# Lower priority for the broadcast of the norms' reciprocal roots

## The chip, the cores and the metric

The kernel runs on one core of a Trainium2 chip. The metric is the device time of one execution in microseconds. Five engines work side by side, each through its own list of instructions: TensorE (PE), VectorE (DVE), ScalarE (ACT), GpSimd (POOL), and SyncE (SP), which here only issues DMAs. An engine takes its instructions strictly in the order of its list; an instruction that waits for a semaphore holds everything behind it on that engine.

## The reference

One decoder layer in float32 over 2048 prompt positions and 8 sample positions (2056 columns), width 1024:

```
h = rmsnorm(x, g_mix);  u, v = split(h @ w_in)                # 1024 -> 512 + 512
y_s5   = glu(gelu(scan_of_complex_state(u)))                  # S5 head group
y_pool = (trailing means of v, windows 2/4/8/16, minus v) @ pool_w * pool_scale
x = x + concat(y_s5, y_pool) @ w_out
h = rmsnorm(x, g_ffn);  x = x + (gelu(gate) * val) @ w_down   # gate, val: causal conv of h @ w_up
y = rmsnorm(x, g_final)
rmsnorm(x, g) = x * rsqrt(mean(x*x, axis=-1) + 1e-6) * g
```

Outputs are y and the new states, in float32.

## The kernel before

The columns of x (positions) lie along the free dimension, the features along the 128 partitions. So a norm needs for each column one number, the reciprocal root of the mean square, in all 128 partitions. `rstd_bcast` (L104 to L123) makes it for a stretch of n columns from the sums of squares, which lie as a 128 x nb tile (position in the partition, block of 128 positions in the column; nb is 2 to 4). VectorE, and ScalarE for the root, work out `rs_r` = the reciprocal root with one Newton step (L110 to L116). Then for each block b VectorE multiplies the identity by the column b of `rs_r`, which gives a diagonal tile `rs_d` (L121, two buffers), and TensorE multiplies a tile of ones by it (L122), which puts the block's numbers as a row into every partition of the PSUM tile `ps_rb`. At last ScalarE copies the n columns of `ps_rb` to SBUF (L123, `rstd`, `rs` or `rs_last`).

This happens 21 times: 5 times in the preparation of x for the input projection (`prep_x`, L253 and L255: stretches of 512, 512, 512, 264 and 256 columns, called SUB 0 to SUB 4 below), 8 times after the out-projection (`norm_out` L946, and L938 for the last stretch), 8 times in the final norm (`final` L1332).

Each fp32 matmul of a projection is done as three matmuls of high and low halves: `mm3` (L87 to L89: high x high, low of the activations x high weights, high x low). The halves are split by ScalarE (a cast, `xh` L79, `wh` L75) and by VectorE or GpSimd (the difference, `xl` L80, `wl` L76). `prep_x` loads `xraw` (three buffers from SUB 2 on), splits it with the gain multiplied in, and gathers the sums of squares.

The stages follow each other: the input projection with the pooling heads and the start of the S5 scan (0 to about 300 us), gates and out-projection with the second half of the scan (to about 600 us), the up-projection of the FFN (to about 1505 us), the down-projection with the final norms (to the end).

The order in which each engine's list is written comes from a scheduler that takes, among the instructions whose inputs would be ready, the one with the lowest priority number. The number (`tc.cur_priority`) counts up by one with every instruction the program emits. Background work, the S5 scan that runs beside the projections, is emitted with BGO = 50 added (`back` L765 to L770 and `s5_ahead` L772 to L777), so that it falls behind foreground work emitted up to 50 instructions later.

Of the kernel before, what the change touches and what calls it, by code (L numbers as in the profile page):

```python
# [40 lines left out]
BGO = 50  # L41
# [3 lines left out]
def build(tc, a):  # L45
# [3 lines left out]
    with es:  # L49
# [54 lines left out]
        def rstd_bcast(ssum, out, n):  # L104
            nb = (n + 127) // 128
            v = misc.tile([128, 8], F32, tag="rs_v", name="rs_v")
            s = misc.tile([128, 8], F32, tag="rs_s", name="rs_s")
            r = misc.tile([128, 8], F32, tag="rs_r", name="rs_r")
            v, s, r = v[:, :nb], s[:, :nb], r[:, :nb]
            V.tensor_scalar(out=v, in0=ssum, scalar1=1.0 / D, scalar2=EPS, op0=ALU.mult, op1=ALU.add)  # L110
            S.activation(out=s, in_=v, func=AF.Sqrt)
            V.reciprocal(out=r, in_=s)
            V.tensor_tensor(out=s, in0=r, in1=r, op=ALU.mult)
            V.tensor_tensor(out=s, in0=s, in1=v, op=ALU.mult)
            V.tensor_scalar(out=s, in0=s, scalar1=-0.5, scalar2=1.5, op0=ALU.mult, op1=ALU.add)
            V.tensor_tensor(out=r, in0=r, in1=s, op=ALU.mult)  # L116
            ps = psm[0].tile([128, 512], F32, tag="ms", name="ps_rb")
            for b in range(nb):
                w = min(128, n - b * 128)
                dg = misc.tile([128, 128], F32, tag="rs_d", name="rs_d")  # L120
                V.tensor_scalar(out=dg[:, :w], in0=ident[:, :w], scalar1=r[:, b:b + 1], scalar2=None, op0=ALU.mult)  # L121
                T.matmul(ps[:, b * 128:b * 128 + w], lhsT=ones, rhs=dg[:, :w], start=True, stop=True)  # L122
            S.copy(out=out, in_=ps[:, :n])  # L123

        def rstd_from(accs, out, n):
            nb = (n + 127) // 128
            ps = psm[0].tile([128, 512], F32, tag="ms", name="ps_st")
            if n % 128:
                V.memset(ps[:, 0:nb], 1.0)
            for b in range(nb):  # L130
                w = min(128, n - b * 128)
                for x, acc in enumerate(accs):
                    T.matmul(ps[0:w, b:b + 1], lhsT=acc[:, b * 128:b * 128 + w], rhs=ones[:, 0:1],
                             start=x == 0, stop=x == len(accs) - 1)
            rstd_bcast(ps[:, 0:nb], out, n)
# [39 lines left out]
        with ExitStack() as er_:  # L175
# [37 lines left out]
            def prep_x(i):  # L213
# [38 lines left out]
                if nat:  # L252
                    rstd_bcast(st(None), rs[:, :n], n)  # L253
                else:
                    rstd_from([acc[:, :n]], rs[:, :n], n)  # L255
# [1226 lines left out]
```

## Time and profile before

| | |
|---|---|
| three runs | 1993.02, 1995.8 (median), 1999.92 us |
| the profiled execution | 1997.34 us, its span 1995.5 us |
| mean granted TensorE clock | 0.973 |
| PE busy | 1877.3 us, 94% of the span |
| DVE, ACT, POOL busy | 1404.4, 898.1, 904.7 us |

The span is the time from the first to the last record of the trace; the 1.84 us between it and the time lie around it. The granted clock is given as a share of full speed. A timeline row gives the start, the duration, the instruction as "out<-in" by the program's names, and in brackets how long its engine was idle before it and what released it. Matmuls overlap, so their pace is read from the distance of their starts, not from their durations.

### The profile page before, as it was taken

How to read it: one execution, taken by the hardware profiler on the slowest of the kernel's cores; microseconds unless marked ns; L12 is line 12 of the kernel's file. 1: busy time of each engine (PE TensorE's matmuls, PEld its weight loads, DVE VectorE, ACT ScalarE, POOL GpSimd, SP SyncE). 2: the span in 40 equal slices, each digit the busy share in tenths (PEclk: the TensorE clock that was granted, in tenths of full speed). 3: DMA queues.
4: the chain of work that ended last, by engine and by line, in shares of the span. 5: the costliest groups of instructions: out<-in, count | busy, mean ns of one | idle time of the engine just before them, and what ended most of it. 6: DMA issues, size and time to landing. Idle time of an engine off the chain costs nothing.

```text
span 1995.5 us, 38363 instructions
## 1 busy us (share of the span) xinstructions
PE 1877.3 (94%) x14680; PEld 1815.0 (91%) x14680; DVE 1404.4 (70%) x2423; ACT 898.1 (45%) x1666; POOL 904.7 (45%) x1091
## 2 busy tenths in 40 slices
PE   6888997999998999999997999999998999999998
PEld 4667876999988999999997999999998989999997
DVE  8888576875588777787789777777775343444675
ACT  5333224544445555555565555555554332322332
POOL 4365662211156455445457555445531165134651
PEclk9989998999999999999998999999998999999999
DMA  6456666865453433233334233323317574356663
GB/s 218 159 165 176 189 179 214 224 176 154 130 178 115 132 122 117 91 112 101 96 102 142 90 114 99 100 87 117 97 60 267 173 248 147 103 189 212 227 205 120
DMA packets 214215, 296.61 MB, mean 149 GB/s; under 512 B 41216, under 2 KB 157824, under 8 KB 213776
## 3 DMA queue, kind: packets, MB, share of 16 engines
q1 hardware_dynamic: 201104, 285.76, 45.3%
q10 hardware_dynamic: 12928, 8.41, 1.5%
q8 instruction: 115, 1.88, 0.4%
q14 instruction: 68, 0.56, 0.1%
HBM read 199.60 MB, written 93.32 MB: 147 GB/s over the span
## 4 chain that ended last, share of the span: by engine, by line
PE 55%; POOL 4%; DVE 4%; DMA 3%; issue 3%; ACT 1%; DVEq 0%; POOLq 0%; ACTq 0%; SPq 0%
PE ps_X L1147 8%; PE ps_X L1146 8%; PE ps_X L1145 8%; PE ps_d L88 4%; PE ps_d L87 4%; PE ps_d L89 4%; PE ps_Z L1146 4%; PE ps_Z L1147 4%; PE ps_Z L1145 4%; PE ps_Y L1147 2%; PE ps_Y L1145 2%; PE ps_Y L1146 2%; DMA x_d<-xo 1%; DMA wr<-w_dn 1%; POOL xo L1307 1%
## 5 line engine op out<-in xcount | busy, mean ns | idle before, releaser
L87 PE MATMUL ps_d<-bh,wh 128*128 128x256 f32 (+1 forms) x1232 | 346.0, 285 | 12.5 <-ACT bh L75 12.5
L88 PE MATMUL ps_d<-bl,wh 128*128 128x256 f32 (+1 forms) x1232 | 349.3, 285 | 6.3 <-DVE bl L76 6.3
L89 PE MATMUL ps_d<-bh,wl 128*128 128x256 f32 (+1 forms) x1232 | 348.5, 284 | 0.0
L76 DVE TENSOR_TENSOR wl<-raw,wh 128x512 fp32r<-128x512 f32 x308 | 270.5, 881 | 64.0 <-ACT wh L75 61.5
L75 ACT CAST wh<-raw 128x512 fp32r<-128x512 f32 x308 | 189.7, 619 | 236.7 <-PE ps_X L1146 166.8
L1173 DVE SCALAR_TENSOR_TENSOR ps_cv<-hup,cst,ps_cv 128x512 f32<-128x512 f32 x352 | 258.1, 750 | 53.1 <-ACT ps_cv L1171 50.9
L1080 POOL TENSOR_TENSOR raw<-raw 128x512 f32<-128x512 f32 x176 | 241.4, 1372 | 83.7 <-DVE wl L76 68.3
L87 PEld LDWEIGHTS ps_d<-bh,wh 128*128 128x128 f32 x1232 | 233.1, 191 | 13.5 <-ACT bh L75 13.5
L88 PEld LDWEIGHTS ps_d<-bl,wh 128*128 128x128 f32 x1232 | 234.7, 191 | 7.4 <-DVE bl L76 7.4
L89 PEld LDWEIGHTS ps_d<-bh,wl 128*128 128x128 f32 x1232 | 235.0, 191 | 0.0
L76 DVE TENSOR_TENSOR bl<-br,bh 128x1536 fp32r<-128x1536 f32 (+3 forms) x56 | 112.4, 2008 | 101.0 <-ACT bh L75 94.0
L1171 ACT ACTIVATE ps_cv<-hup,cst 128x512 f32<-128x512 f32 x176 | 135.9, 782 | 8.3 <-DVE hup L1133 3.9
L87 PE MATMUL ps_in<-xh,wh 128*128 128x512 f32 (+2 forms) x288 | 110.0, 383 | 10.4 <-ACT xh L79 8.1
L926 POOL TENSOR_TENSOR acc<-acc,sq 128x256 f32<-128x256 f32 (+1 forms) x56 | 44.5, 794 | 150.9 <-ACT sq L925 148.6
L88 PE MATMUL ps_in<-xl,wh 128*128 128x512 f32 (+2 forms) x288 | 106.0, 368 | 6.7 <-DVE xl L80 6.7
L1100 POOL TENSOR_TENSOR tt<-cv 128x256 f32<-128x256 f32 (+1 forms) x88 | 79.8, 915 | 61.6 <-DVE cv L1180 28.0
L75 ACT CAST bh<-br 128x1536 fp32r<-128x1536 f32 (+3 forms) x56 | 76.6, 1376 | 66.5 <-PE ps_d L89 65.9
L89 PE MATMUL ps_in<-xh,wl 128*128 128x512 f32 (+2 forms) x288 | 104.3, 363 | 0.1
L1147 PE MATMUL ps_X<-b11h,wl 128*128 128x256 f32 (+1 forms) x352 | 100.0, 284 | 3.1 <-DVE wl L76 3.1
L1146 PE MATMUL ps_X<-b11l,wh 128*128 128x256 f32 (+1 forms) x352 | 99.9, 284 | 2.9 <-DVE b11l L76 2.9
L1145 PE MATMUL ps_X<-bt2h,wh 128*128 128x256 f32 (+1 forms) x352 | 99.9, 284 | 2.5 <-ACT p L1128 2.5
L1146 PE MATMUL ps_Y<-b21l,wh 128*128 128x256 f32 (+1 forms) x352 | 99.3, 282 | 2.5 <-DVE b21l L76 2.5
(436 smaller groups left out, 6476.5 us busy)
## 6 DMA issues: line engine op xcount, KB each, us to landing
raw<-w_up SPq DMA_DIRECT2D x176, 256.0 KB
wr<-w_dn SPq DMA_DIRECT2D x36, 704.0 KB
op_d<-tt SPq DMA_DIRECT2D x33, 512.0 KB
br<-op_d SPq DMA_DIRECT2D x21, 768.0 KB
br<-op_d SPq DMA_DIRECT2D x21, 640.0 KB
op_d<-cv SPq DMA_DIRECT2D x33, 256.0 KB
wr<-w_in SPq DMA_DIRECT2D x16, 512.0 KB
tab<-tab_d SPq DMA_DIRECT2D x32, 256.0 KB
```

The lines of the kernel that those rows point to most:

```text
L75: S.copy(out=hi, in_=src)
L76: (eng or V).tensor_tensor(out=lo, in0=src, in1=hi.bitcast(F32), op=ALU.subtract)
L87: T.matmul(ps, lhsT=wh, rhs=rh, start=k == 0, stop=False)
L88: T.matmul(ps, lhsT=wh, rhs=rl, start=False, stop=False)
L89: T.matmul(ps, lhsT=wl, rhs=rh, start=False, stop=k == K - 1)
L1080: P.tensor_tensor(out=r, in0=x, in1=y, op=op)
L1100: P.tensor_tensor(out=o, in0=x, in1=y, op=ALU.subtract)
L1145: T.matmul(ps, lhsT=wh[:, k], rhs=hh[:, k], start=first and k == 0, stop=False, skip_group_check=not first)
L1146: T.matmul(ps, lhsT=wh[:, k], rhs=hl[:, k], start=False, stop=False, skip_group_check=not first)
L1147: T.matmul(ps, lhsT=wl[:, k], rhs=hh[:, k], start=False, stop=k == 3, skip_group_check=not first)
L1171: S.activation(out=c, in_=h[:, o:o + 512], func=AF.Identity, scale=tap(2, jj), bias=col(C_CB, jj))
L1173: V.scalar_tensor_tensor(out=c, in0=h[:, o - 2 + k:o + 510 + k], scalar=tap(k, jj), in1=c, op0=ALU.mult, op1=ALU.add)
```

## The change

In `rstd_bcast` the PSUM tile, the diagonal tiles, the broadcast matmuls and ScalarE's copy are emitted with the background's 50 added to the priority, and then the counter is set back to where it stood before these instructions. Nothing that is computed changes, and no instruction is added or taken away.

```diff
             V.tensor_tensor(out=r, in0=r, in1=s, op=ALU.mult)
+            p_ = tc.cur_priority
+            tc.cur_priority = p_ + BGO
             ps = psm[0].tile([128, 512], F32, tag="ms", name="ps_rb")
             for b in range(nb):
                 w = min(128, n - b * 128)
...
                 V.tensor_scalar(out=dg[:, :w], in0=ident[:, :w], scalar1=r[:, b:b + 1], scalar2=None, op0=ALU.mult)
                 T.matmul(ps[:, b * 128:b * 128 + w], lhsT=ones, rhs=dg[:, :w], start=True, stop=True)
             S.copy(out=out, in_=ps[:, :n])
+            tc.cur_priority = p_
 
         def rstd_from(accs, out, n):
```

So the scheduler writes the lists in another order. TensorE's list differs in two stretches only, rows 363 to 703 (about 130 to 230 us of the trace before) and rows 1164 to 2075 (about 300 to 430 us), and by two matmuls of the down-projection that change places. The broadcasts of SUB 0 and SUB 1 stand where they stood; of the 16 later ones two change their place between the matmuls around them (the first and the second after the out-projection). Names with a line number in the changed kernel are 2 higher at L121 to L123 and 3 higher from there on.

TensorE, input projection, before: blocks 3 and 4 of SUB 2's norm (`ps_rb` from `rs_d` 1424 and 1427) stand in the middle of a unit of the projection (`ps_in` 1477).

```order
L88 MATMUL ps_in_1477<-xl_378,wh_1186 128x512
L89 MATMUL ps_in_1477<-xh_377,wl_1187 128x512
L87 MATMUL ps_in_1477<-xh_386,wh_1186 128x512
L122 MATMUL ps_rb_1417<-rs_d_1424,ones_132 128x128
L122 MATMUL ps_rb_1417<-rs_d_1427,ones_132 128x128
L88 MATMUL ps_in_1477<-xl_387,wh_1186 128x512
L89 MATMUL ps_in_1477<-xh_386,wl_1187 128x512
L87 MATMUL ps_in_1477<-xh_395,wh_1186 128x512
```
Now at this place stand blocks 1 and 2 (1418 and 1421), which before stood some 30 rows earlier:

```order
L89 MATMUL ps_in_1477<-xh_386,wl_1187 128x512
L87 MATMUL ps_in_1477<-xh_395,wh_1186 128x512
L88 MATMUL ps_in_1477<-xl_396,wh_1186 128x512
L124 MATMUL ps_rb_1417<-rs_d_1418,ones_132 128x128
L89 MATMUL ps_in_1477<-xh_395,wl_1187 128x512
L87 MATMUL ps_in_1477<-xh_404,wh_1186 128x512
L124 MATMUL ps_rb_1417<-rs_d_1421,ones_132 128x128
L88 MATMUL ps_in_1477<-xl_405,wh_1186 128x512
```
and blocks 3 and 4 stand behind the next unit's (`ps_in` 1626) fourth and fifth tile:

```order
L87 MATMUL ps_in_1626<-xh_1362,wh_1616 128x512
L88 MATMUL ps_in_1626<-xl_1363,wh_1616 128x512
L124 MATMUL ps_rb_1417<-rs_d_1424,ones_132 128x128
L89 MATMUL ps_in_1626<-xh_1362,wl_1617 128x512
L87 MATMUL ps_in_1626<-xh_1371,wh_1616 128x512
L124 MATMUL ps_rb_1417<-rs_d_1427,ones_132 128x128
L88 MATMUL ps_in_1626<-xl_1372,wh_1616 128x512
```
What moved: blocks 3 and 4 went 23 and 25 rows back, behind the rest of `ps_in` 1477, a matmul of the pooling heads (`ps_z` 1512) and eleven matmuls of the next unit. SUB 3's last block (`rs_d` 1610) goes back as well, from row 446 to row 473.

VectorE beside it, before: both diagonal tiles stand ahead of the split of SUB 2's sixth tile (`xl` 1381); `xl` of L80 are the splits, `rt` and `ra` a table for the scan, `pl`, `vt`, `csum` the pooling heads.

```order
L673 SCALAR_TENSOR_TENSOR pl_1294<-wsum_1292,vt_1286 128x512
L279 TENSOR_TENSOR ra_1305<-rt_1304,ns_680 128x4x32 x2
L280 TENSOR_TENSOR rt_1304<-rt_1304,nc_679 128x8x32
L121 TENSOR_SCALAR rs_d_1424<-ident_145,rs_r_1409 128x128
L121 TENSOR_SCALAR rs_d_1427<-ident_145,rs_r_1409 128x128
L80 SCALAR_TENSOR_TENSOR xl_1381<-xraw_1378,cst_134,xh_1380 128x512
L676 TENSOR_TENSOR pl_1294<-wsum_1292,icn_285 128x16
```
Now the split 1381 follows on `rt` at once, and seven rows on the diagonal tiles stand behind the eighth tile's split (`xl` 1399):

```order
L665 SCALAR_TENSOR_TENSOR csum_1460<-ones_132,vt_1456 128x528
L80 SCALAR_TENSOR_TENSOR xl_1390<-xraw_1387,cst_134,xh_1389 128x512
L285 TENSOR_TENSOR rt_1304<-rt_1304,ra_1305 128x4x64 x2
L80 SCALAR_TENSOR_TENSOR xl_1399<-xraw_1396,cst_134,xh_1398 128x512
L123 TENSOR_SCALAR rs_d_1424<-ident_145,rs_r_1409 128x128
L676 SCALAR_TENSOR_TENSOR pl_1464<-wsum_1462,vt_1456 128x512
L123 TENSOR_SCALAR rs_d_1427<-ident_145,rs_r_1409 128x128
```
What moved: the two diagonal tiles went behind the splits 1381, 1390 and 1399. SUB 3's last one (1610) now stands behind `xl` 1588, the last split of SUB 3; before it stood ahead of six of the eight.

ScalarE in the out-projection, before: `wo` are weights that are cast, `yg` the scan's activation, `sg` the sigmoid of the gate that frees a PSUM tile, `gh` the high halves for the out-projection.

```order
L75 CAST wo0h_3207<-wo0r_3205 128x1024
L606 COPY bus_280<-psw_3472 128x32
L639 ACTIVATE yg_3498<-psy_3499 128x544
L75 CAST wo1h_3213<-wo1r_3211 128x1024
L898 ACT_TABLE_LOAD
L898 ACTIVATE sg_3294<-ps_g_3281 128x256
L898 ACTIVATE sg_3314<-ps_g_3301 128x256
L75 CAST gh4_3259<-zr_3257 128x256
```
Now a weight's cast stands ahead of `yg`, and two casts `gh` stand ahead of the sigmoids:

```order
L75 CAST wo0h_3207<-wo0r_3205 128x1024
L609 COPY bus_280<-psw_3472 128x32
L75 CAST wo1h_3213<-wo1r_3211 128x1024
L642 ACTIVATE yg_3498<-psy_3499 128x544
L75 CAST gh4_3259<-zr_3257 128x256
L75 CAST gh5_3265<-zr_3263 128x256
L901 ACT_TABLE_LOAD
L901 ACTIVATE sg_3294<-ps_g_3281 128x256
L901 ACTIVATE sg_3314<-ps_g_3301 128x256
```
What moved: `gh4` and `gh5` went ahead of the first sigmoid. At the next stretch of columns the two casts go ahead as well, a square and a cast of another kind too, and a second pair of table load and `yg` now stands between the last sigmoid and `gh3`.

## Rows read from the trace of the kernel before

**Rows 1.** The page: span, and TensorE's busy time.
```profile
span 1995.5 us, 38363 instructions
...
PE 1877.3 (94%) x14680; PEld 1815.0 (91%) x14680; DVE 1404.4 (70%) x2423; ACT 898.1 (45%) x1666; POOL 904.7 (45%) x1091
```

**Rows 2.** Windows: length, PE, PEld, DVE, ACT, POOL busy, PEclk, DMA share, GB/s.
```profile
140.00:150.00 10.00, 7.41 (x22) 5.75 (x23) 10.00 (x20) 4.41 (x8) 7.22 (x4) 0.66 0.87 273
170.00:180.00 10.00, 8.21 (x60) 7.07 (x59) 8.55 (x19) 4.69 (x8) 1.71 (x4) 1.00 0.49 148
200.00:250.00 50.00, 50.00 (x333) 43.95 (x333) 26.91 (x46) 11.22 (x19) 31.87 (x41) 1.00 0.66 186
320.00:330.00 10.00, 6.71 (x33) 5.92 (x33) 9.39 (x19) 7.39 (x17) 2.12 (x1) 0.78 0.72 241
```

**Rows 3.** Waits of PE, 300 to 640 us: total us, times, longest.
```profile
PE ps_rb L122 <- DVE rs_d L121: 8.0, 3, 4.8
PE psy L638 <- DVE H L619: 4.0, 1, 4.0
PE ps_g L87 <- ACT sg L898: 3.1, 3, 2.1
```

**Rows 4.** Timeline of PE: start us, us, instruction, [idle before <- releaser].
```profile
138.07 0.40 PE L89 MATMUL ps_in<-xh,wl 128*128 128x512 f32 x1
138.30 0.39 PE L87 MATMUL ps_in<-xh,wh 128*128 128x512 f32 x1
142.59 1.22 PE L122 MATMUL ps_rb<-rs_d,ones 128*128 128x128 f32 x4 [3.89 <-DVE rs_d L121]
143.46 0.77 PE L88 MATMUL ps_in<-xl,wh 128*128 128x512 f32 x1
...
147.87 0.48 PE L89 MATMUL ps_in<-xh,wl 128*128 128x512 f32 x1
```

**Rows 5.** Timeline of DVE beside it (same columns).
```profile
140.18 2.55 DVE L121 TENSOR_SCALAR rs_d<-ident,rs_r 128x128 f32<-128x128 f32 x2
...
144.46 0.16 DVE L677 TENSOR_TENSOR pl<-pl,vt 128x16 f32<-128x16 f32 x1
...
148.38 1.24 DVE L114 TENSOR_TENSOR rs_s<-rs_s,rs_v 128x2 f32<-128x2 f32 x1
149.54 0.74 DVE L80 SCALAR_TENSOR_TENSOR xl<-xraw,cst,xh 128x512 fp32r<-128x512 f32 x1
150.20 0.47 DVE L121 TENSOR_SCALAR rs_d<-ident,rs_r 128x128 f32<-128x128 f32 x2
```

**Rows 6.** Timeline of POOL beside it.
```profile
138.23 4.22 POOL L76 TENSOR_TENSOR wl<-wr,wh 128x1024 fp32r<-128x1024 f32 x1 [1.33 <-ACT wh L75]
...
147.29 2.31 POOL L665 TENSOR_TENSOR wsum<-csum 128x512 f32<-128x512 f32 x1 [0.16 <-DVE csum L662]
```

**Rows 7.** All rs_d, durations ns min/median/max, first and last start.
```profile
L121 DVE TENSOR_SCALAR rs_d<-ident,rs_r x51: 231/280/2357, 35.9 to 1987.6; 128x128 f32<-128x128 f32 x48, 128x8 f32<-128x8 f32 x3
```

**Rows 8.** Last split of the preparation: DVE, PE; waits of ACT, 128 to 176.
```profile
176.03 0.49 DVE L80 SCALAR_TENSOR_TENSOR xl<-xraw,cst,xh 128x256 fp32r<-128x256 f32 x1
...
176.57 0.38 PE L88 MATMUL ps_in<-xl,wh 128*128 128x256 f32 x1 [0.21 <-DVE xl L80]
...
ACT xh L79 <- DMA xraw<-xT: 27.5, 15, 4.4
```

**Rows 9.** PE in the out-projection, at a wait for the sigmoid.
```profile
321.44 0.39 PE L87 MATMUL ps_g<-yh,wg3h 128*128 128x256 f32 x1 [2.13 <-ACT sg L898]
```

**Rows 10.** ACT in the out-projection, next stretch: table load, yg, gh.
```profile
348.57 1.28 ACT L639 ACT_TABLE_LOAD   x1
349.86 0.63 ACT L639 ACTIVATE yg<-psy 128x544 f32<-128x544 f32 x1
350.38 0.40 ACT L75 CAST gh<-zr 128x256 fp32r<-128x256 f32 x1
```

**Rows 11.** PE at a later broadcast, in the out-projection.
```profile
583.17 1.19 PE L122 MATMUL ps_rb<-rs_d,ones 128*128 128x128 f32 x4 [4.82 <-DVE rs_d L121]
```

## Prediction

> **What bounds the kernel now.** I read the head of the page first. TensorE is busy for 1877.3 us of a span of 1995.5 us [rows 1], so all that any order of work can give back is the 118 us in which it idles, and the stretches in which its clock is down. The windows show where that is. From 200 to 250 us TensorE has no idle time (50.00 of 50) at full clock; in 140 to 150 us it is busy for 7.41 of 10 us at a mean granted clock of 0.66, and in 320 to 330 us for 6.71 at 0.78 [rows 2]. Then I read the waits of TensorE, since the change touches only what TensorE waits for at `ps_rb`, and whatever moves around it. In the out-projection and at its end the broadcasts cost three waits of 8.0 us together, the longest 4.8 [rows 3]; in the input projection the timeline has one of 3.89 us [rows 4]. Of the other waits of the out-projection, 4.0 us go to the scan (`psy` on `H`) and 3.1 us to the sigmoids (`ps_g` on `sg`) [rows 3].
>
> Last I compared these places with the new lists. The wait of 3.89 us stands at blocks 3 and 4 of SUB 2's norm, which move. The one of 4.8 us [rows 11] stands at a broadcast after the out-projection that keeps its neighbours on every engine, and so do the other two of the 8.0 us. The change can therefore touch two stretches: the input projection around 130 to 230 us, by the wait itself, and the out-projection around 300 to 430 us, by the order that results there. The FFN keeps its order but for two matmuls that change places.
>
> **Input projection: what goes.** TensorE starts the last matmul before the broadcast at 138.30 and the broadcast at 142.59, after 3.89 us of idling for `rs_d` [rows 4]. VectorE has both diagonal tiles in hand from 140.18 for 2.55 us [rows 5], where the median of one is 280 ns and the longest of all 51 is 2357 ns [rows 7]: this is the one that was held up, and it ends with GpSimd's `wl`, which runs from 138.23 for 4.22 us [rows 6]. After the wait the clock is down: eleven matmuls start 0.44 us apart (from 143.46 to 147.87), where before it they start 0.23 us apart (138.07, 138.30) [rows 4]. That loses 11 x 0.21 = 2.3 us. Gross, 3.9 + 2.3 = 6.2 us are at stake here.
>
> **What comes instead.** TensorE now runs through the place of the wait. After 138.30 it does eleven more matmuls and two broadcast blocks (the old pair took 0.87 us, 142.59 to 143.46, at the low clock [rows 4], so 0.45 at the full one), and so comes to the pooling matmul `ps_z` 1512 at about 138.3 + 2.5 + 0.5 = 141.3. `ps_z` needs the last instruction on `pl` 1294 (144.46, 0.16 us [rows 5]). VectorE's list up to it is 2.55 us shorter by the two diagonal tiles [rows 5], so that `pl` is ready at 142.1 and TensorE waits 0.8 us. With `ps_z` (512 columns of the same kind as the pair's 256, so twice its 0.45) and eleven matmuls (2.5) it stands at block 3 at 145.5. The diagonal tile is ready later: it stands behind the split 1399, which was at 149.54 [rows 5]. Of what was ahead of that split the two diagonal tiles (2.55) go, and so do the small instructions of the next norm, of which the step at 148.38 took 1.24 us [rows 5]: 3.8 together. The tile ends at 149.54 - 3.8 + 0.74 + 0.28 [rows 5, 7] = 146.8, a wait of 1.3 us. The next tile stands one pooling instruction further, about a split's 0.74 us [rows 5], of which one matmul covers 0.23: another 0.5. New waits: 0.8 + 1.3 + 0.5 = 2.6 us. They come in three pieces instead of one, and I take the clock as not falling. At about 147 us TensorE would be 6.2 - 2.6 = 3.6 us ahead.
>
> **How much of it lasts.** SUB 3's last block (`rs_d` 1610) now stands behind the last split of SUB 3, `xl` 1588, so TensorE idles there for some 3 to 4 us that it did not idle before. This is not simply a cost: the matmuls behind it need the splits of SUB 3 and SUB 4 anyway. The end of the whole preparation is the split at 176.03, for which TensorE waits at 176.57, the last such wait [rows 8]; what decides is when that split comes. It hangs on ScalarE, which waits for the loads [rows 8], and a load starts when a split has freed one of three buffers. The splits move up by the 2.55 us of the two diagonal tiles [rows 5], and the loads with them. In 170 to 180 us TensorE still idles for 1.8 us [rows 2], so the lead is not capped by its own work there, and from 200 us on it is full [rows 2], so the lead stays. I take 2.5 us of gain, the shift of the splits, rather than the lead of 3.6, which the wait for the last split caps. The bounds: the whole 6.2 us are gained if the new waits fall where TensorE would wait anyway; at the other end the loads do not move up and the new wait at `rs_d` 1610 is a second one of 3.9 us with its 2.3 us of low clock: 6.2 - 2.6 - 6.2, a loss of 2.6 us.
>
> Here the Trainium skill speaks. Its page "SBUF — State Buffer", section "Who interferes with whom", has it that a `tensor_scalar` of VectorE can enter a mode in which it needs the ports that it shares with GpSimd, and that whoever began first holds them for its whole instruction. The rows agree: the 2357 ns tile ends with `wl`. By that rule the moved tile is not safe either, since it stands close behind `csum`, with which GpSimd's `wsum` begins (147.29, 2.31 us long [rows 6]); it would be held for what is left of `wsum` once the two splits between them (0.74 each [rows 5]) are done, at most 2.31 - 1.48 = 0.8 us. By the rule the gain would be 2.5 - 0.8 = 1.7 us, by the pair at 150.20, which took 0.47 us for two tiles with no GpSimd work beside it in the trace [rows 5], 2.5 us.
>
> **Out-projection.** Here no broadcast that moves has a wait of its own; the second one even moves up. What changes is ScalarE's order. Two casts `gh`, 0.40 us each [rows 10] and overlapping by 0.1, now precede the sigmoid for which TensorE waits 2.13 us at 321.44 [rows 9]: +0.7 us. At the next stretch a square and a copy also precede it, +0.4 to +1.1. Against this the scan's matmuls and VectorE's steps stand some 5 us earlier, of whose 4.0 us wait [rows 3] a part goes. I take zero, between -4.0 and +4.
>
> **The sum.** The profiled execution took 1997.34 us, 1.84 us more than its span [rows 1]. 1997.34 - 2.5 + 0 = 1994.8; the median of the runs shown lies 1.5 us below the profiled one, so a typical run is expected between 1993.3 and 1994.8. I say 1994.
>
> **Rivals.**
> (a) Faster than that. The order around the broadcast was the cause of both losses, and they go: 6.2 us in the input projection, and in the out-projection half of the 7.1 us of waits for the scan and the sigmoids [rows 3], 3.5 us. 1997.3 - 9.7 = 1987.6. For it: the clock of 0.66 [rows 2] is a loss that only the wait explains. Against it: the new place of block 3 still lies ahead of its diagonal tile.
> (b) Slower, by ScalarE in the out-projection. The sigmoid frees the PSUM tile that `ps_g` needs; the casts put ahead cost 0.7 us at the first stretch and 1.1 at the next, and there a table load and a `yg`, 1.28 + 0.63 us [rows 10], now stand ahead of `gh3`, the last input of the first `ps_o`: 1.9. Together 3.7 us; each of two such waits is followed by matmuls at the lower clock as after the wait at 142 us, 2 x 2.3 = 4.6. With no gain in the input projection: 1997.3 + 8.3 = 2005.6. It decides from the point at which the wait before `ps_g` at 321.44 grows above 3 us. For it: the mean clock there is already 0.78 [rows 2]. Against it: ScalarE idles in that stretch for a quarter of the time (7.39 of 10 busy [rows 2]).
> (c) The change hardly does what it says. 5 of 21 broadcasts move, none of them one that the 8.0 us [rows 3] are lost at, and the preparation stays bound by its loads: 1996 to 1998.
>
> **The numbers.** Forecast 0.45, (a) 0.25, (b) 0.15, (c) 0.15. About 0.3%, 6 us, is what a measurement of this kernel can tell from no change. Faster by more than that (under 1989.8): 0.22 of (a) and 0.08 of the forecast's tail, 0.30. Slower (over 2001.8): 0.13 of (b), 0.05 from the tails of the forecast and (c), 0.18. The same: 0.52. The likeliest case alone spans 1990 to 1999; the range reaches to most of (a) and of (b), 1985 to 2004.
>
> **What would show it.** Right: no wait over 3 us at `ps_rb` before 150 us, one of 1 to 2 us at 145 to 148, the clock of that stretch at about 0.9, and the split now at 176.03 at about 173.5. Wrong: a broadcast's wait of 3 us or more at a lower clock at about 160 us, that split at 176 or later, or waits of `ps_g` for `sg` that add up to more than 5 us. All of it is wrong if the FFN, whose order stands, differs by more than 2 us between the traces.

## The result and the profile after

The changed kernel takes 2007.1 us (median of 7 runs, 2002.06 to 2014.19), the kernel before 1993.28 us (7 runs, 1991.29 to 1999.92): a ratio of 1.0071, 95% interval 1.0055 to 1.0087. It is slower by about 14 us, above the range. The profiled execution took 2002.06 us, the lowest of its seven, its span 1.86 us less.

Ahead of everything else stands where on the way it falls behind. The first matmul of each stage marks it (us from the span's start; gates and out-projection begin with `ps_g`, the up-projection with `ps_X`, the down-projection with `ps_d`):

| | first `ps_g` | first `ps_X` | first `ps_d` | end |
|---|---|---|---|---|
| before | 298.4 | 598.7 | 1512.9 | 1995.5 |
| after | 300.4 | 607.8 | 1524.7 | 2000.2 |
| later by | 2.0 | 9.1 | 11.8 | 4.7 |

So between these two traces 2.0 us are lost in the input projection and 7.1 in the out-projection. The 2.0 are rather too little: in the six traces whose input projection has the order of before (before, and e8, e10, e11, e12, e14 of the experiments below) the first `ps_g` stands at 294.3 to 298.4 us, on average at 296.3; in the nine with the changed order (after, e3, e7, e9, e13, e15 to e18) at 297.8 to 301.5, on average at 299.7, which is 3.4 us later. The FFN's order is the same but for two matmuls that change places; the up-projection took 912.1 to 918.0 us over the twenty traces of this study, so its 2.7 are within what it varies by. The last stage took 482.6 us in the trace before, the longest of all; the others have 475.6 to 481.0. That stage alone brings these two spans from 11.8 us apart to 4.7; the medians lie 13.8 apart.

The page after, span and TensorE [rows 1]:

```profile
span 2000.2 us, 38361 instructions
...
PE 1873.6 (94%) x14680; PEld 1813.7 (91%) x14680; DVE 1410.1 (70%) x2423; ACT 898.8 (45%) x1666; POOL 901.9 (45%) x1091
```
TensorE works 3.7 us less than before and idles 8.4 us more. The windows after (columns as in [rows 2]), with two more stretches, 165 to 174 and 340 to 360 us:

```profile
140.00:150.00 10.00, 5.28 (x22) 3.38 (x20) 10.00 (x18) 2.04 (x4) 5.12 (x4) 1.00 0.91 272
...
165.00:174.00 9.00, 8.26 (x56) 8.26 (x57) 8.25 (x17) 3.29 (x8) 1.27 (x1) 0.81 0.34 95
...
170.00:180.00 10.00, 9.40 (x74) 8.84 (x72) 9.88 (x20) 3.70 (x8) 1.41 (x3) 0.99 0.38 110
...
320.00:330.00 10.00, 5.27 (x21) 4.55 (x21) 9.91 (x18) 8.74 (x17) 2.35 (x1) 0.66 0.87 274
...
340.00:360.00 20.00, 14.15 (x108) 13.54 (x107) 13.13 (x23) 9.86 (x17) 8.61 (x11) 0.95 0.59 176
```
and these two before:

```profile
165.00:174.00 9.00, 6.91 (x49) 5.95 (x48) 8.86 (x15) 4.15 (x10) 0.82 (x3) 1.00 0.36 105
...
340.00:360.00 20.00, 19.27 (x164) 19.05 (x162) 13.75 (x29) 12.39 (x24) 9.21 (x11) 1.00 0.71 198
```
In 140 to 150 us the clock is back at 1.00 from 0.66 (about 0.9 was forecast), and yet TensorE gets as many matmuls done as before, 22: its busy time shrank because each is shorter, and idle time took the place. But this trace is alone in that: over 140 to 152 us the other eight with the changed order have a clock of 0.72 to 0.86, and the six with the order of before 0.72 to 0.86 as well. And in 165 to 174 us the clock is down, 0.81 from 1.00; it is at 0.62 to 0.81 there in six of the nine with the changed order, and at 1.00 in five of the six with the order of before. In 340 to 360 us TensorE gets 108 matmuls done instead of 164.

**Input projection.** TensorE after (start, duration, instruction, idle time before it):

```profile
144.58 1.13 PE L700 MATMUL ps_z<-pl,pw__287 128*128 128x512 f32 x2 [2.97 <-DVE pl L680]
...
150.28 0.49 PE L124 MATMUL ps_rb<-rs_d,ones 128*128 128x128 f32 x2 [2.04 <-DVE rs_d L123]
...
165.74 0.39 PE L124 MATMUL ps_rb<-rs_d,ones 128*128 128x8 f32 x2 [2.40 <-DVE rs_d L123]
```
The wait of 3.89 us at 142.59 [rows 4] is gone; three stand for it, 7.4 us together, and the low clock of 165 to 174 us comes behind the last of them. VectorE beside it, and then GpSimd:

```profile
140.51 2.85 DVE L80 SCALAR_TENSOR_TENSOR xl<-xraw,cst,xh 128x512 fp32r<-128x512 f32 x1
...
144.37 0.16 DVE L680 TENSOR_TENSOR pl<-pl,vt 128x16 f32<-128x16 f32 x1
...
147.54 1.83 DVE L285 TENSOR_TENSOR rt<-rt,ra 128x256 f32<-128x256 f32 x2
149.29 0.74 DVE L80 SCALAR_TENSOR_TENSOR xl<-xraw,cst,xh 128x512 fp32r<-128x512 f32 x1
149.96 0.28 DVE L123 TENSOR_SCALAR rs_d<-ident,rs_r 128x128 f32<-128x128 f32 x1
```
```profile
138.52 4.29 POOL L76 TENSOR_TENSOR wl<-wr,wh 128x1024 fp32r<-128x1024 f32 x1 [1.29 <-ACT wh L75]
...
147.12 1.64 POOL L668 TENSOR_TENSOR wsum<-csum 128x512 f32<-128x512 f32 x1 [1.86 <-DVE csum L665]
```
The diagonal tiles are no longer held up: all 51 take 225 to 1318 ns, median 281, where the longest took 2357 [rows 7]. But the split that took their place in VectorE's list takes 2.85 us instead of its usual 0.74: it ends 0.55 us behind GpSimd's `wl` (142.81), as the first of the tiles ended 0.08 us behind it before (142.45) [rows 5, 6]. The same happens a second time. Before, the small `rs_s` at 148.38 took 1.24 us and ended with GpSimd's `wsum` [rows 5, 6]; now `rs_s` is gone from there, and two `rt`, which took 0.75 us before, take 1.83 while `wsum` runs. So `pl` comes at 144.37 as before (144.46), and the split that was at 149.54 at 149.29: hardly anything moved up. The end of the preparation moves back, from 176.03 [rows 8] to 178.43, with TensorE waiting for it:

```profile
178.43 0.49 DVE L80 SCALAR_TENSOR_TENSOR xl<-xraw,cst,xh 128x256 fp32r<-128x256 f32 x1
```
```profile
178.97 0.39 PE L88 MATMUL ps_in<-xl,wh 128*128 128x256 f32 x1 [0.36 <-DVE xl L80]
```
It is SUB 2's move that does this: that split stands at 177.99 in e1, where SUB 2 alone moves, and at 174.41 in e2, where SUB 3 alone does.

**Out-projection.** TensorE's waits after, 300 to 640 us (total, times, longest), against [rows 3]:

```profile
PE ps_rb L124 <- DVE rs_d L123: 11.2, 4, 4.7
PE ps_g L87 <- DVE x L923: 5.9, 3, 4.7
PE psy L640 <- ACT yg L642: 4.2, 2, 2.8
PE psy L641 <- DVE H L622: 4.0, 1, 4.0
...
PE ps_g L87 <- ACT sg L901: 1.5, 1, 1.5
```
The sigmoids cost less than before (1.5 for 3.1). Two things are new, `ps_g` on the residual add `x`, which frees its PSUM tile, and a wait at the first broadcast after the out-projection, which had none before. The longest of the one, and the other:

```profile
357.70 0.41 PE L87 MATMUL ps_g<-yh,wg2h 128*128 128x256 f32 x1 [4.75 <-DVE x L923]
...
393.68 0.68 PE L124 MATMUL ps_rb<-rs_d,ones 128*128 128x128 f32 x4 [2.51 <-DVE rs_d L123]
```
To see where the wait for `x` comes from one follows it back through the engines. SyncE (start, duration of the issue) before, and after:

```profile
334.66 0.37 SPq L866 DMA_DIRECT2D wo5r<-w_out  x1
336.63 1.26 SPq L566 DMA_DIRECT2D tab<-tab_d  x2
...
343.13 0.33 SPq L866 DMA_DIRECT2D wo7r<-w_out  x1
```
```profile
337.16 0.61 SPq L569 DMA_DIRECT2D tab<-tab_d  x1
337.87 1.45 SPq L869 DMA_DIRECT2D wo5r<-w_out  x1
...
348.52 0.33 SPq L869 DMA_DIRECT2D wo7r<-w_out  x1
```
A load of the scan's table now stands ahead of the weight `wo5r`, which is issued 3.2 us later; 2.0 of these are the later start of the stage. ScalarE after, then VectorE after and before:

```profile
344.98 1.05 ACT L75 CAST wo5h<-wo5r 128x1024 fp32r<-128x1024 f32 x1 [8.86 <-DMA wo5r<-w_out]
...
346.56 0.17 ACT L609 COPY bus<-psw 128x32 f32<-128x32 f32 x1
...
356.84 0.62 ACT L642 ACTIVATE yg<-psy 128x544 f32<-128x544 f32 x1
```
```profile
346.75 0.69 DVE L603 TENSOR_TENSOR t<-psw,tab 64x512 f32<-64x512 f32 x1 [6.64 <-ACT bus L609]
347.46 0.68 DVE L604 TENSOR_TENSOR t<-psw,tab 64x512 f32<-64x512 f32 x1
348.18 0.42 DVE L923 TENSOR_TENSOR x<-ps_o,xt 128x256 f32<-128x256 f32 x1
...
357.22 0.42 DVE L923 TENSOR_TENSOR x<-ps_o,xt 128x256 f32<-128x256 f32 x1
```
```profile
344.01 0.75 DVE L920 TENSOR_TENSOR x<-ps_o,xt 128x256 f32<-128x256 f32 x2 [4.89 <-DMA xt<-xT]
344.69 1.23 DVE L76 TENSOR_TENSOR wo6l<-wo6r,wo6h 128x1024 fp32r<-128x1024 f32 x1
347.62 0.42 DVE L920 TENSOR_TENSOR x<-ps_o,xt 128x256 f32<-128x256 f32 x1 [1.70 <-DMA xt<-xT]
348.07 0.69 DVE L600 TENSOR_TENSOR t<-psw,tab 64x512 f32<-64x512 f32 x1
```
Before, ScalarE's cast of `wo5` starts at 339.60. After, it waits 8.86 us for the load; the scan's `bus` stands behind it, the scan's steps `t` on VectorE wait for `bus`, and the residual adds stand among and behind these steps, where before they stood ahead of them. The add at 357.22 is the one for which TensorE idles 4.75 us; `yg`, at 349.86 before [rows 10], comes at 356.84. The scan's steps themselves are no later than before (346.75 against 348.07, the second pair 353.62 against 354.71): what changed for the adds is that they stand behind these steps. Some 1.8 of the 4.75 us are two small steps `gx` just ahead of the add, which take 1.46 and 0.67 us beside GpSimd's `wo7l` (354.14, 2.35 us long) and took 0.16 and 0.15 before.

None of the broadcasts that move stands between 340 and 360 us; the order there is a knock-on of the scheduler. It comes out the same, with the two broadcasts that move behind it, when none of the later broadcasts is lowered (e1 below). Two questions follow: is it this order or the input projection that costs the time, and if the order, which part of it.

### The profile page after: what moved, and what is told of

It reads as the page before. It is cut to its first block, busy times and chain, and to the rows that moved or that the text cites. A ratio compares the mean times of both kernels' runs of the same rounds, so it can differ in the third digit from the quotient of the medians.

```text
span 2000.2 us, 38361 instructions
## 1 busy us (share of the span) xinstructions
PE 1873.6 (94%) x14680; PEld 1813.7 (91%) x14680; DVE 1410.1 (70%) x2423; ACT 898.8 (45%) x1666; POOL 901.9 (45%) x1091
## 5 line engine op out<-in xcount | busy, mean ns | idle before, releaser
L1150 PE MATMUL ps_Z<-bt3h,wl 128*128 128x256 f32 (+1 forms) x352 | 99.9, 284 | 2.1 <-DVE wl L76 2.1
```

The source lines that it names most:

```text
L1150: T.matmul(ps, lhsT=wl[:, k], rhs=hh[:, k], start=False, stop=k == 3, skip_group_check=not first)
```

## The experiments

The theories that the expectations speak of: A, the late `wo5` behind the table's load; B, the waits of the moved broadcasts in the input projection; C, almost any other order of the out-projection is worse than that of the kernel before; and, for the last six, VectorE's order of residual adds and scan's steps. All runs of an experiment are compared with runs of the kernel before on the same chip. The two last columns are from each one's trace: the first `ps_g`, and from there to the first `ps_X`.

| | ratio to before | 95% interval | first `ps_g` | out-projection |
|---|---|---|---|---|
| before | | | 298.4 | 300.3 |
| after | 1.0071 | 1.0055 to 1.0087 | 300.4 | 307.4 |
| e1_sub2_only | 1.0078 | 1.0065 to 1.0090 | 300.4 | 310.9 |
| e2_sub3_only | 1.0035 | 1.0019 to 1.0051 | 295.3 | 303.9 |
| e3_tab_later | 1.0042 | 1.0027 to 1.0056 | 297.8 | 300.7 |
| e4_all_but_sub23 | 1.0005 | 0.9994 to 1.0015 | 297.8 | 303.3 |
| e5_offset60 | 1.0041 | 1.0029 to 1.0054 | 301.1 | 309.1 |
| e6_offset100_prep | 1.0073 | 1.0052 to 1.0094 | 296.8 | 313.9 |
| e7_change_3_raw | 1.0086 | 1.0069 to 1.0103 | 299.7 | 314.1 |
| e8_before_3_raw | 1.0054 | 1.0035 to 1.0073 | 294.3 | 312.7 |
| e9_change_wo5_pool | 1.0049 | 1.0033 to 1.0064 | 298.9 | 313.8 |
| e10_before_tab_later | 1.0005 | 0.9990 to 1.0019 | 295.6 | 303.0 |
| e11_before_zr_later | 0.9985 | 0.9970 to 0.9999 | 295.2 | 299.9 |
| e12_before_tab_earlier | 1.0004 | 0.9989 to 1.0018 | 297.2 | 304.8 |
| e13 (new input, old out-projection) | 1.0014 | 0.9998 to 1.0030 | 300.0 | 303.8 |
| e14 (old input, new out-projection) | 1.0041 | 1.0025 to 1.0058 | 297.1 | 310.7 |
| e15_change_old_dve_order | 1.0039 | 1.0024 to 1.0053 | 299.5 | 303.5 |
| e16_change_old_load_order | 1.0016 | 1.0000 to 1.0031 | 301.0 | 300.1 |
| e17_change_old_sync_queue | 1.0110 | 1.0087 to 1.0133 | 298.9 | 323.6 |
| e18_change_adds_first | 1.0101 | 1.0073 to 1.0129 | 301.5 | 313.8 |

### Which broadcasts: e1, e2, e4

```diff
-        def rstd_bcast(ssum, out, n):
+        def rstd_bcast(ssum, out, n, bg=0):
...
+            p_ = tc.cur_priority; tc.cur_priority = p_ + bg
...
-                    rstd_bcast(st(None), rs[:, :n], n)
+                    rstd_bcast(st(None), rs[:, :n], n, BGO * (i == 2))
```
This is e1; e2 has `i == 3`, and e4 has 50 at every broadcast but those two.

> The lowered priority for the broadcast of SUB 2 alone. ScalarE's and SyncE's lists come out the same as with the whole change; TensorE's and VectorE's differ from it only around SUB 3's broadcast. Theory A (the loss is a knock-on: the out-projection's lists come out in another order, in which a table load of the scan stands ahead of the load of wo5 on SyncE and the weights come some 5 us late): as slow as the whole change but for at most 3 us, so 6 to 14 us above before, the first ps_g wait for x around 355 us again 3 us or more. Theory B (the loss is the broadcasts' own new waits in the input projection, the last one of SUB 3 above all): that wait is gone here, and the time is within 3 us of before.

> The lowered priority for the broadcast of SUB 3 alone. In the input projection only that broadcast moves; in the out-projection wo5 stands ahead of the table load on SyncE, as before. Theory A: within 3 us of before. Theory B: SUB 3's late wait (2.4 us in the changed kernel) is there, so 2 to 10 us above before.

> The lowered priority for all broadcasts but those of SUB 2 and SUB 3. The lists of VectorE, ScalarE and SyncE are those of before, on TensorE four transposes change places with neighbours. Theories A and B alike: within 3 us of before. Were it slower by 6 us or more, the 16 later broadcasts or something that no list shows (the addresses of tiles) would be the cause.

SUB 2 alone makes the whole loss (1.0078), with the changed kernel's order of the out-projection; all 19 others without SUB 2 and 3 make none (1.0005), with the order of before. In e2, where SUB 2's tiles stay, they are held up as before and not the split (VectorE of e2):

```profile
139.69 2.56 DVE L121 TENSOR_SCALAR rs_d<-ident,rs_r 128x128 f32<-128x128 f32 x2
142.16 0.74 DVE L80 SCALAR_TENSOR_TENSOR xl<-xraw,cst,xh 128x512 fp32r<-128x512 f32 x1
```
In e4 VectorE's order is that of before, and yet a split is held up and the tiles are not. `wl` begins at 138.65 there, as this split does; before it began when the split was under way (138.23 and 138.17), and the tiles were next (VectorE of e4):

```profile
138.66 2.88 DVE L80 SCALAR_TENSOR_TENSOR xl<-xraw,cst,xh 128x512 fp32r<-128x512 f32 x1
...
142.80 0.47 DVE L121 TENSOR_SCALAR rs_d<-ident,rs_r 128x128 f32<-128x128 f32 x2
```
The time held up goes with `wl`, not with the tiles. Where e2's 1.0035 comes from is open: neither stage of its trace is late by more than 4 us. Its order of the out-projection is a third one, neither that of before nor that of the changed kernel, and e5 has the same and e3 nearly so; these three stand at 1.0035, 1.0041 and 1.0042. That points to this order, but no run has it with the input projection of before.

### Other offsets: e5, e6

60 at every broadcast instead of 50, and 100 at those of `prep_x` alone.

```diff
-            tc.cur_priority = p_ + BGO
+            tc.cur_priority = p_ + 60
```

> The whole change with 60 in place of 50. In the input projection the broadcasts stand a few rows on from where 50 puts them; in the out-projection the lists come out in the other order, with wo5 ahead of the scan's table load on SyncE. Theory A (knock-on order in the out-projection, late wo5): 4 to 8 us above before, as with the tables put later (1997.7), so 6 to 10 us faster than with 50. Theory B (the broadcasts' own waits): as with 50, 12 to 15 us above before, since these waits stay.

> 100 in place of 50, in the preparation alone (the other calls keep their old priority). In the out-projection all lists but TensorE's and some of VectorE's come out as with 50, a table load ahead of wo5. Theory A: 11 to 16 us above before, as the change. Theory B: further back means other waits in the input projection, so another loss, by 3 us or more either way.

Neither is as fast as before. e5 loses about 8 us, near the 4 to 8 of theory A and well under the 12 to 15 of theory B, and `wo5r` is issued ahead of the table there, as A supposed; but in its trace the out-projection takes 309.1 us, no less than in the changed kernel. e6 is the more telling: its first `ps_g` is earlier than in the trace before, 296.8, and its loss is whole. The order of the input projection need not lose anything for the out-projection to take 313.9 us.

### The late load: e3, e9, e10, e12

e3 puts the table's loads of the scan's second half 50 later, so that `wo5r` is issued first; e9 has GpSimd issue `wo5r`; e10 and e12 put the table's loads 50 later and 20 earlier in the kernel before.

```diff
+                    q_ = tc.cur_priority; tc.cur_priority = q_ + (50 if half == 1 else 0)
                     Y.dma_start(out=tab[h * 64:h * 64 + 64], in_=tab_d[qd // 2]...
+                    tc.cur_priority = q_
```
```diff
-                Y.dma_start(out=raw, in_=src)
+                (P if tag == "wo5" else Y).dma_start(out=raw, in_=src)
```

> The whole change, and besides the loads of the scan's tables in the second half at a priority 50 later, so that SyncE issues wo5 ahead of the table as before; the input projection stands as in the changed kernel but for the lists behind 300 us. Theory A: the 7 us of the out-projection come back, and what stays is the input projection's share, 2 to 3 us above before (ratio 1.000 to 1.002). Theory B: 8 to 14 us above before, as with the change.

> The whole change, with one DMA moved: the load of the raw wo5 is issued by GpSimd, right behind its split of wo3 that frees the buffer, and not by SyncE behind the scan's table load. ScalarE's list is that of the changed kernel up to the second stretch of the out-projection, TensorE's up to row 1326. Theory A (the late wo5 is what the out-projection of the changed kernel loses): 3 to 6 us faster than the change, 8 to 11 us above before, and the wait of ps_g for x near 357 us gone. Theory C (not this load but the order as a whole, ScalarE's and VectorE's casts with it): 12 us or more above before, with another wait in place of that one.

> The kernel before, no broadcast moved, with the scan's table loads of the second half at a priority 50 later: the input projection's lists stand as they were, those of the out-projection come out in another order, with wo5 ahead of the table load as before. Theory A: within 3 us of before. Theory C (in the out-projection nearly every other order is worse than the one that the kernel before has): 3 to 12 us above before.

> The kernel before, no broadcast moved, with the scan's table loads of the second half at a priority 20 earlier: again only the out-projection's lists change (and one place of the down-projection), wo5 stays ahead of the table load. Theory A: within 3 us of before. Theory C: 3 to 12 us above before. If it is faster, the order of before is not the end of what reordering gives, and the knock-on of the change could have fallen either way.

e3's trace has the out-projection's time back, 300.7 us, as theory A has it. But this trace is the fastest of its seven runs, and the ratio, 1.0042 or about 8 us, is above A's range and at the lower end of B's; it settles nothing.

e9's time, about 10 us above before, lies in theory A's range, but the wait that A said would go stays. `wo5`'s cast is back at 339.57, and the adds stand behind the scan's steps. VectorE of e9, and TensorE, which waits for that add:

```profile
351.24 1.98 DVE L580 TENSOR_TENSOR gi<-gi,gx 128x4 f32<-128x4 f32 x1
353.25 0.69 DVE L600 TENSOR_TENSOR t<-psw,tab 64x512 f32<-64x512 f32 x1
...
354.67 0.42 DVE L920 TENSOR_TENSOR x<-ps_o,xt 128x256 f32<-128x256 f32 x1
```
```profile
355.15 0.39 PE L87 MATMUL ps_g<-yh,wg2h 128*128 128x256 f32 x1 [4.04 <-DVE x L920]
```
So the late load is not needed for that wait, and theory A alone falls. So does theory C: e10 and e12 have other orders of the out-projection at no cost (1.0005, 1.0004).

### Other inputs: e7, e8, e11

Three buffers for the raw weights instead of two, in the changed kernel and in the one before; and in the one before the loads of `zr` 20 later.

```diff
-            cr = ecr.enter_context(tc.tile_pool(name="cr", bufs=2, side="right", reuse_waits="tile"))
+            cr = ecr.enter_context(tc.tile_pool(name="cr", bufs=3, side="right", reuse_waits="tile"))
```

> The whole change, with three buffers in place of two for the raw output-projection weights, so that wo5 and wo6 are issued ahead of the table loads without waiting for the split of the weights before. Theory A: the loss of the out-projection goes, and more if the loads bound it before as well: -4 to +6 us against before. Theory B: 12 us above before.

> The kernel before with three buffers for the raw output-projection weights; no priority is lowered. If the chain of these loads bounds TensorE between 320 and 350 us there too, 2 to 8 us faster than before; if not, within 2 us.

> The kernel before, no broadcast moved, with the loads of the pooling head's outputs (zr) 20 later: only the out-projection's lists change, from TensorE's row 1282 on. Theory A: within 3 us of before. Theory C: 3 to 12 us above before.

A third buffer slows the kernel before too, by as much as most of the change: its lists come out otherwise. Both expectations missed, and neither run tells anything of the buffers. e11 is the only kernel that is faster than before, and just so (0.9985, to 0.9999); among eighteen intervals of 95% one such proves nothing.

### Each stage's order with the other's: e13, e14

Here the lists are held by hand. Edges that only fix the order on one engine, and add no wait, hold the out-projection's part of all five lists to the order of the other kernel; outside that part nothing changes.

```diff
-        build(tc, aps)
+        build(tc, aps); hold(tc, nc)
...
+def hold(tc, nc):
+    by = {i.name: i for i in nc.cur_bb.bb.instructions}
...
+    for o in ORDER.values():
+        for p, c in zip(o, o[1:]):
+            tc.add_manual_dep(by[f"I-{c}"], f"I-{p}", info, reason="order")
```

> The change whole, but every engine is held to the order of the kernel before in the out-projection (about 300 to 430 us); only the input projection keeps the changed order. Theory 'order of the out-projection': most of the loss is made there, so this kernel takes 1993 to 1997, at most the 2.5 us or so that the moved SUB 2 costs by the first ps_g. Theory 'input projection': the new waits there make the loss, and it stays, 2004 to 2008.

> The kernel before, but every engine is held to the changed kernel's order in the out-projection; no broadcast of the input projection moves. Theory 'order of the out-projection': 2001 to 2006. Theory 'input projection': 1993 to 1996.

This settles the first question. The new order of the out-projection in the kernel before costs 1.0041; the change with the old one is at 1.0014, an interval that just takes in no change. Together 1.0055, the lower end of the change's own interval; that the input projection has a share at all is seen in the traces (3.4 us, above) rather than in this ratio. The stretch 340 to 360 us, e13 and e14:

```profile
340.00:360.00 20.00, 20.00 (x154) 20.00 (x155) 12.91 (x24) 9.65 (x17) 8.44 (x10) 0.90 0.63 194
```
```profile
340.00:360.00 20.00, 15.89 (x121) 15.52 (x120) 15.10 (x27) 11.60 (x21) 9.13 (x12) 0.91 0.62 193
```
With the old order TensorE is busy without a break, with the new one for 15.89 of 20 us, though the input projection of e14 is not late (297.1). Behind this stretch e14 also has the changed kernel's wait at a broadcast, 2.11 us at 390.87.

### Which list of the out-projection: e15 to e18

The same edges for one list: in e15 VectorE's and in e16 SyncE's and ScalarE's to the old order, the others left to the scheduler. In e17 all lists as in the changed kernel but SyncE's as before; in e18 all as in the changed kernel, but the three adds and `wo6l` ahead of the scan's steps.

> The change, with VectorE alone held to its old order in the out-projection (residual adds ahead of the scan's steps); the other engines' lists are laid around it by the scheduler. If VectorE's order is what makes TensorE wait for x there: 1994 to 1998. If the loads' order on SyncE does: 2002 to 2007.

> The change, with SyncE and ScalarE held to their old order in the out-projection (wo5 and wo7 loaded and cast where they were); VectorE and TensorE are laid around it by the scheduler. If the loads' order makes the loss: 1994 to 1998. If VectorE's order does: 2002 to 2007.

> The change, every list of the out-projection as in the changed kernel, but SyncE issues its loads and stores there in the order of the kernel before (wo5 ahead of the scan's table). Theory 'load order': wo5h's cast returns to about 340 us, and the kernel takes 1994 to 1997. Theory 'VectorE's order': the residual adds still stand behind the scan's steps and ps_g still waits for x after 345 us: 2001 to 2006.

> The change, every list of the out-projection as in the changed kernel, but on VectorE the three residual adds x and the split of wo6 that stand among the scan's steps at 346 to 357 us are put ahead of the first of these steps, as in the kernel before; the loads stay late. Theory 'VectorE's order': the waits of ps_g for x go, and it takes 1995 to 1999. Theory 'load order': the cast of wo5h and with it the scan's input are still late, the loss stays, 2003 to 2007.

e15 and e16 recover half of the loss and most of it, but around the held list the scheduler drew the other in question (SyncE's in e15, VectorE's in e16) back near the old order as well, so they don't part the two. e17 and e18 do, and both theories fail: either half of the old order alone is slower than none, 1.0110 and 1.0101. Why is seen in e18. TensorE's waits, 301 to 460 us, and VectorE:

```profile
PE psy L637 <- ACT yg L639: 11.4, 3, 6.2
```
```profile
349.39 0.42 DVE L920 TENSOR_TENSOR x<-ps_o,xt 128x256 f32<-128x256 f32 x1 [6.57 <-DMA xt<-xT]
...
351.52 0.41 DVE L920 TENSOR_TENSOR x<-ps_o,xt 128x256 f32<-128x256 f32 x1
353.88 0.42 DVE L920 TENSOR_TENSOR x<-ps_o,xt 128x256 f32<-128x256 f32 x1 [1.95 <-DMA xt<-xT]
354.34 0.69 DVE L600 TENSOR_TENSOR t<-psw,tab 64x512 f32<-64x512 f32 x1
```
The wait for `x` is down to 0.4 us in 338 to 366 us, but the adds wait for `xt`. The first waits 6.57 us for one that SyncE issues behind the table and `wo5r`, at 342.85 (338.58 before); the last waits 1.95 us for one behind `wo7r` (349.85 there, 343.13 before). The scan's steps now wait behind the adds, and `yg` with them: 11.4 us instead of 4.2. In e17 `wo5`'s cast is at 342.34 and `wo7r` at 345.86, and the adds behind the scan's steps; it waits 8.7 us for `yg`, and loses most later, between 405 and 472 us, for which I have no single cause. So I take it that the adds' place on VectorE and the loads' place on SyncE belong together. That is argued: no run puts back these two and nothing else; e16, with both near the old order and ScalarE's too, comes nearest (1.0016).

## Why the prediction was wrong

**The step that failed first** is "The splits move up by the 2.55 us of the two diagonal tiles". I took the 2.55 us as time of the tiles, which goes with them. They were time of `wl`: one instruction of VectorE beside it waits for its end, be it a tile or a split, while those ahead of that one take their usual time (a split at 138.51 took 0.73 us). With the tiles gone the next one, a split, took 2.85 us. The 1.24 us of `rs_s`, the other part of "3.8 together", were time of `wsum` in the same way, and 1.08 of them came back at `rt`. The text weighed the rule of the Trainium skill, page "SBUF — State Buffer", section "Who interferes with whom", for the tiles alone. The same section says that a VectorE instruction with two SBUF inputs contends with a GpSimd instruction that reads SBUF; the split has two, `xraw` and `xh`, and the trace agrees, with 2.85 us beside `wl` and 0.74 elsewhere. No run here takes `wl` away; that the held time is its own is read from e4 and from when the held instructions end (last section). So of the forecast gain of 2.5 us nothing came.

**The new waits.** Forecast 0.8 at `ps_z`, then 1.3 and 0.5; they are 2.97 and 2.04, and at SUB 3's last block, where 3 to 4 were named and set against waits that would fall anyway, 2.40. "I take the clock as not falling" failed too: in eight of the nine traces with this order it falls in 140 to 152 us as it did before, and in six behind SUB 3's last block. That is the case that the bound of a loss of 2.6 us was built on, a second wait with its low clock, there with 3.9 us. The bound came about right. The loss is 2.0 at the first `ps_g` in the trace, 3.4 on average over the traces, and 1.0014 (0.9998 to 1.0030), about 3 us, as a whole in e13.

**The larger step** is the term of the out-projection, "I take zero, between -4.0 and +4". It is +7.1 us in the trace and 1.0041 (1.0025 to 1.0058) by itself, about 8 us. I had compared ScalarE's new list with TensorE's waits, and not SyncE's and VectorE's; there a load moved past another and the residual adds moved behind the scan's steps, for which TensorE waits 5.9 us in the changed kernel. And "no broadcast that moves has a wait of its own" did not stay so: the first one behind the out-projection has one of 2.51 us in its new place.

**The rivals.** (b) comes near in its number, 2005.6, but by luck, for the mechanism is another: the wait at 321.44 [rows 9], which was to grow above 3 us, is 1.47 at 323.44, and the waits for `sg` shrank. (a) fell: the order around the broadcast went, but the waits came back at its neighbours, and the low clock with them in most traces. (c) was right in that the longest of the broadcasts' waits hardly changes (4.82 at 583.17 [rows 11], 4.68 at 592.75 after), though together they grow from 8.0 to 11.2, and wrong in taking the order around them as free.

**The signs.** One sign of being wrong came, the last split at 178.43, past 176; the two others did not, with 2.40 us at a broadcast at 165.74 and 1.5 us of waits for `sg`. The sign that would have made all of it wrong, the FFN off by more than 2 us, was set too tight: its two stages differ by 2.7 and 7.0 us between these traces, and they vary by nearly as much where their order is the same (last section).

**Open:** which of the waits before the last split moves it, e2's 1.0035, e3's ratio against its trace, the later loss of e17, and about 2 us between the trace's 11.8 at `ps_d` and the medians' 13.8.

## What to carry to other kernels

An instruction that a neighbour on another engine holds up does not own that time: before counting it as a gain, ask what stands next in its list, and whether that is held as well. Where a scheduler lays the lists, a priority in one stage can lay another anew: compare the lists of every engine, the one that only issues loads too, in every stage that differs, and follow each moved load to who waits for it. An order is tested whole: here the change cost 0.7% with both moved pieces, and 1.0 to 1.1% with either of them put back alone.

## What the runs showed of the hardware

- Full clock is not progress: in 140 to 150 us TensorE did 22 matmuls at 0.66 (before) and 22 at 1.00 (after).
- The time for which GpSimd holds up VectorE belongs to GpSimd's instruction. In all twenty traces `wl` at 138 us ends 2.27 to 2.38 us behind the start of the VectorE instruction that is held up, and that one ends just behind `wl`: a tile in seven traces, 0.08 to 0.09 us behind, a split in thirteen, 0.55 us behind. `wl` takes 2.36 to 2.44 us at its other places and up to 4.29 here, so it seems to wait for VectorE first; that much is read from the durations alone.
- The same list does not take the same time: with the order of before in both, the last stage took 482.6 us in the trace before and 476.3 in e10's, and with one order of the up-projection it took 912.1 us in e6's and 918.0 in e3's. So two spans 5 us apart say little of a change; the stage marks and the ratios say more.
